# A trunk of dense blocks and a recurrence on one core: the recurrence starts after the seventh dense block, and the loads of its post-processing move behind a later chunk

## The chip, the cores and the metric

The kernel runs on one core of a Trainium2 chip. The metric is the device time of one execution, in microseconds (us), as the median of three runs. Every product is an fp32 product made of three faster ones: a matrix is split into a high part (hi) and a rest (lo), and hi·hi, hi·lo and lo·hi are summed.

## The reference, cut to what matters

Two residual layers over 1024 tokens of 1024 features. Layer 0 mixes with a gated MLP and pools, layer 1 with a recurrence over time (below); each is followed by a SwiGLU block with 2816 hidden features.

```python
def wkv7_scan(r, w, k, v, a, b):
    def step(state, inp):
        r_t, w_t, k_t, v_t, a_t, b_t = inp
        sa = jnp.einsum('bhvk,bhk->bhv', state, a_t)
        state = (state * w_t[:, :, None, :] + sa[..., None] * b_t[:, :, None, :]
                 + v_t[..., None] * k_t[:, :, None, :])
        return state, jnp.einsum('bhvk,bhk->bhv', state, r_t)
    _, ys = lax.scan(step, s0, xs)

# around it, per token and head
y = ((y - mean) * lax.rsqrt(var + GN_EPS)).reshape(bsz, seq, d)
y = y * ln_w + ln_b
y = (y + bonus.reshape(bsz, seq, d)) 
return (y * g) @ w_o, v_first

def swiglu(hn, w_gate, w_up, w_down):
    return (jax.nn.silu(hn @ w_gate) * (hn @ w_up)) @ w_down
```

## The kernel before, in words

The 1024 tokens are worked in two halves of 512, h = 0 and 1. The recurrence is computed in chunks of 64 tokens, eight per half, as matrix products of 64 by 64 within a chunk and a state handed from chunk to chunk. `recur(h, wp)` is its code. It runs in two phases, one for each half, and in each it is interleaved with dense work: `drive` takes steps of a SwiGLU generator (`ffn`) and, by a ratio of 3, steps of the recurrence. Each `yield` of the recurrence names a cost; a dense block (one 128-feature slice: 24 matmuls of 128 by 512, eight triples by `mm3`) counts 1, and so earns a cost of 3. PE's order is the order in which the code is written (and thus the costs at the `yield`s decide it); the order of the other engines is found by a planner that simulates the program's time. DVE, ACT and the queues run in order.

The dense blocks are of three kinds: gate (`sg`: the silu of its result), up (its result times `sg` gives `hidhi`, `hidlo`) and down (`wdhi`, `wdlo` times `hidhi`, `hidlo`, added to `h`). The weights of a block come by one load of 512 KB into `raw` (three buffers), issued on ACT's queue; ACT makes `whi` or `wdhi` of it, DVE `wlo` or `wdlo`.

SP's queue issues the loads of the recurrence. `load(c)` brings `ar`, `bk`, `uv` and `XT` of a chunk; `bk` has one buffer. `with_reload` puts four loads of two slices of `h` (512 KB each) between the first steps. `gram(c, q)` is 32 products of `ar` and `bk`, which DVE masks into `gt`; `flip_bk` transposes `bk`; `below` and `below2` finish the triangular inverse in `XT`; `burst(c)` then chains the products of a chunk: `Q`, then `uv`, then the new state `S`, with the two grams of the next chunk in between. `post(jj)` normalizes two finished chunks: it reads `lnw` (the weights of the norm), `vch` (v of the two chunks) and `gch` (the gate), makes `ysb`, and transposes it on PE. The order of the products of the recurrence on PE is kept by `ordered`, which puts each behind the last.

`tc.issue_after(i)` has an instruction stand behind instruction i in the order of the program; it is no wait for a result.

Of the kernel before, what the change touches and what calls it, by code (L numbers as in the profile page):

```python
# [16 lines left out]
P = 128  # L17
# [13 lines left out]
LOWRANK_AT, GATE_AT, MIX_AT = (5, 8), (7, 8), 2  # L31

BURST = 12.0

BESIDE = (4, 2)

# [2 lines left out]
def tile_trunk(  # L39
# [8 lines left out]
    act, dve, pool, pe, sp = nc.scalar, nc.vector, nc.gpsimd, nc.tensor, nc.sync  # L48
# [25 lines left out]
    def bc(ap, shape):  # L74
        return ap.to_broadcast(shape)
# [20 lines left out]
    def col(c):  # L96
        return vec[:, c : c + 1]
# [35 lines left out]
    def take(key):  # L133
        i = pos[0]
        assert plan[i][0] == key, (plan[i][0], key)
        pos[0] += 1
        split_at(i)
        load_at(i + 1)
        if i + 1 in raws:
            load_at(i + 2)  # L140
        split_at(i + 1)
        return ready.pop(i)
# [186 lines left out]
    def mmt():  # L329
        return pst("mm")  # L330

    def auxt():
        return pst("aux")
# [6 lines left out]
    def hsl(h):  # L340
        return slice(h * HT, (h + 1) * HT)

    def mm3(o, whi, wlo, xhi, xlo, first, last):
        pe.matmul(o, whi, xhi, start=first, stop=False)  # L344
        pe.matmul(o, whi, xlo, start=False, stop=False)  # L345
        pe.matmul(o, wlo, xhi, start=False, stop=last)  # L346

    def rsqrt(t):
        pool.tensor_tensor(out=t, in0=t, in1=mhalf[:, : t.shape[1]], op=ALU.pow)  # L349
# [125 lines left out]
    o = auxt()  # L475
# [3 lines left out]
    o = auxt()  # L479
# [19 lines left out]
    for h in range(2):  # L499
        ops = [mmt() for _ in range(4)]  # L500
        for kp in range(4):
            with tc.issue_after(x_issued):
                whi, wlo = take(("v0", h, kp))
            whi, wlo = (w.rearrange("p (k m) -> p k m", k=2) for w in (whi, wlo))
            xhi, xlo = hn[h]
# [25 lines left out]
    o = auxt()  # L531
# [36 lines left out]
    for m in ORD_Z:  # L568
        g = m - 8
        whi, wlo = take(("in", m))  # L570
        win = WINS[g]
        prev = None
        for h in range(2):
            o = mmt()
# [15 lines left out]
            while w < win:  # L590
                n = l0.tile([P, 16 + HT], F32, tag="zw", bufs=2, name="zw")
                b0 = base + w
# [12 lines left out]
    for m in range(4):  # L605
        whi, wlo = take(("in", m))
        for h in range(2):
            o = mmt()
# [7 lines left out]
    for h in range(2):  # L616
        hi, lo = act_tiles((xlp, actp)[h])
        ys.append((hi, lo))
        for k in (4, 5, 6, 7, 0, 1, 2, 3):
            src = zt[k - 4, h] if k >= 4 else mx[:, k, hsl(h)]  # L620
# [135 lines left out]
    g_d = [dram.tile([P, KT, HT], F32, name=f"g_d{h}") for h in range(2)]  # L756
    xi_d = [dram.tile([2, 8, 2, 8, 32, 2, 32], F32, name=f"xi_d{h}") for h in range(2)]
# [31 lines left out]
    rows = [slice(0, 64), slice(64, 128)]  # L789
# [354 lines left out]
    def recur(h, wp):  # L1144
# [5 lines left out]
        def wt(tag, bufs, shape):  # L1150
            return wp.tile(shape, F32, tag=tag, bufs=bufs, name=tag)
# [2 lines left out]
            return pst("sm").rearrange("p (a b) -> p a b", b=64)  # L1154

        lnw = wt("lnw", 1, [P, 8, 64])
        for r in range(2):
            act.dma_start(
                lnw[rows[r]], rwkv_ln_w[0].rearrange("(p r d) -> r p d", r=2, d=64)[r].partition_broadcast(64)
            )  # L1160
        C, ypair = {}, {}
        S, Q, last = [state_d], {}, []

        def ordered(f, *args, **kw):
# [16 lines left out]
        def load(c):  # L1181
            ar = wt("ar", 2, [P, 8, 2, 64])
            sp.dma_start(ar, ar_d[h][c])
            bk = wt("bk", 1, [P, 8, 2, 64])
            sp.dma_start(bk, bk_d[h][c])
            uv = wt("uv", 2, [P, 8, 2, 64])
            vs = v_d[h][c * 64 : c * 64 + 64]
            sp.dma_start(uv[64:128, :, 0, :], vs[:, 0])
            sp.dma_start(uv[0:64, :, 1, :], vs[:, 1])

            xx = wt("XT", 2, [P, 8, 96])
            x1, XT = xx[:, :, 0:32], xx[:, :, 32:96]
            for r in range(2):
                b0 = r * 64
                sp.dma_start(
                    xx[b0 : b0 + 32, :, 0:64], xi_d[h][0, :, r, c].rearrange("p i a j -> i p (a j)")
                )
                sp.dma_start(XT[b0 + 32 : b0 + 64, :, 32:64], xi_d[h][1, :, r, c, :, 1].rearrange("p i j -> i p j"))
                pool.memset(XT[b0 + 32 : b0 + 64, :, 0:32], 0.0)
            gt = wt("gt", 2, [P, 8, 2, P])  # L1200
            C[c] = (ar, bk, uv, gt, x1, XT)

        def gram(c, q):
            ar, bk, _, gt, _, _ = C[c]
            og = [pst("sm").rearrange("p (a b) -> p a b", b=P) for _ in range(2)]
            for j in range(4):
                p = q * 4 + j
                for b in range(2):
                    for r in range(2):
                        mm(  # L1210
                            og[r][rows[b], j, :], bk[rows[r], p, b, :],
                            ar[rows[r], p].rearrange("p a b -> p (a b)"), start=True, stop=True,
                        )
            for r in range(2):
                dve.tensor_tensor(
                    out=gt[:, q * 4 : q * 4 + 4, r, :], in0=og[r], in1=bc(gm.unsqueeze(1), [P, 4, P]), op=ALU.mult
                )
# [110 lines left out]
        def post(jj):  # L1328
            yp = ypair[0]
            j = h * 4 + jj  # L1330
            gch = wt("gch", 1, [P, 8, P])
            sp.dma_start(gch, g_d[h][:, :, jj * P : (jj + 1) * P])
            vch = wt("vch", 1, [P, 2, 8, 64])
            for r in range(2):
                sp.dma_start(
                    vch[rows[r]].rearrange("t c p d -> t c (p d)"),
                    v_d[h][jj * P : (jj + 1) * P, r].rearrange("(c t) p d -> t c (p d)", t=64),
                )
            v16 = vch.rearrange("t c p d -> t (c p) d")
            b16 = bon[:, 2 * j : 2 * j + 2, :].rearrange("t c p -> t (c p)")  # L1340
            pool.tensor_tensor(out=v16, in0=v16, in1=bc(b16.unsqueeze(2), [P, 16, 64]), op=ALU.mult)
            st = wt("st", 1, [P, 2, 8, 6])
            for r in range(2):
                for p in range(8):
                    dve.bn_stats(out=st[:, r, p, :], in_=yp[:, r, p, :])
            sts = st.rearrange("p a b s -> p (a b) s")
            mean, dm, var = (wt(n, 1, [P, 16]) for n in ("mean", "dm", "var"))
            me, mo, ve, vo = (sts[:, :, i] for i in (1, 4, 2, 5))
            dve.tensor_tensor(out=mean, in0=me, in1=mo, op=ALU.add)
            dve.tensor_tensor(out=dm, in0=me, in1=mo, op=ALU.subtract)  # L1350
            dve.tensor_tensor(out=var, in0=ve, in1=vo, op=ALU.add)
            dve.scalar_tensor_tensor(out=dm, in0=dm, scalar=16.0, in1=dm, op0=ALU.mult, op1=ALU.mult)
            dve.tensor_tensor(out=var, in0=var, in1=dm, op=ALU.add)
            dve.tensor_scalar(out=var, in0=var, scalar1=1.0 / 64, scalar2=GN_EPS, op0=ALU.mult, op1=ALU.add)
            rsqrt(var)
            dve.scalar_tensor_tensor(out=mean, in0=mean, scalar=-0.5, in1=var, op0=ALU.mult, op1=ALU.mult)
            yield 0.3
            ysb = wt("ysb", 1, [P, 2, 8, 64])
            for r in range(2):
                for p in range(8):  # L1360
                    i = r * 8 + p
                    act.activation(
                        ysb[:, r, p, :], yp[:, r, p, :], AF.Identity, scale=var[:, i : i + 1], bias=mean[:, i : i + 1]
                    )
            yield 0.3
            for q, eng in enumerate((dve, pool)):
                eng.tensor_tensor(out=ysb[:, q], in0=ysb[:, q], in1=lnw, op=ALU.mult)
                eng.tensor_tensor(out=ysb[:, q], in0=ysb[:, q], in1=vch[:, q], op=ALU.add)
            yield 0.3
            yield 0.3  # L1370
            for q in range(2):
                o = pst("sm")
                for i in range(4):
                    p = 4 * q + i // 2 * 2
                    ordered(
                        pe.transpose, o[:, i * P : (i + 1) * P], ysb[:, i % 2, p : p + 2, :].rearrange("t p d -> t (p d)"), ident
                    )
                ov = o.rearrange("p (q c r t) -> p q r c t", q=2, c=2, r=2)
                for i in range(4):
                    m = q * 4 + i  # L1380
                    g = gch[:, m, :].rearrange("p (c t) -> p c t", c=2)
                    dve.scalar_tensor_tensor(
                        out=g, in0=ov[:, i // 2, i % 2], scalar=col(C_LNB + m), in1=g, op0=ALU.add, op1=ALU.mult,
                    )
                yield 0.5
            sp.dma_start(y_d[h][:, :, jj * P : (jj + 1) * P], gch)

        load(0)
        load(1)
        yield 0.2  # L1390
        gram(0, 0)
        yield 0.5
        gram(0, 1)
# [4 lines left out]
        for c in range(8):  # L1398
            bkt, w1 = yield from burst(c, bkt, w1)
            yield BURST / 2  # L1400
            if c % 2 == 1:
                yield from post(c // 2)
            yield BURST / 2

# [219 lines left out]
```

## Time and profile before

| | |
|---|---|
| median of three runs | 2525.26 us (2524.75 to 2525.75) |
| the profiled execution | 2522.66 us |
| its span | 2520.9 us, mean granted clock of PE 0.983 |
| PE busy | 2432.2 us (96%) |
| DVE, ACT, POOL busy | 1401.8, 890.7, 299.8 us |
| moved by DMA | 310.69 MB, mean 123 GB/s |
| phase 1 of the recurrence, h = 0 | about 927 to 1240 us |
| phase 2, h = 1 | about 1669 to 1940 us |

A row of the profile gives start, length, engine, line of the kernel, operation, output <- inputs, and in brackets the idle time ahead of it with what ended it. Engines with a q (ACTq, SPq) are their queues, on which DMAs are issued. Buffer numbers are left out in the profile; in the order of the program they stand behind the names.

### The profile page before, as it was taken

The page shows a single profiled execution, that of the slowest core. Times are in us where ns is not written, and L with a number is a line of the kernel's source. Part 1 is how long each engine was busy: PE and PEld are TensorE (multiplying, and loading weights), DVE is VectorE, ACT ScalarE, POOL GpSimd, SP SyncE. Part 2 cuts the span into 40 slices and gives each one's busy share as a digit, 9 for nine tenths or more (in the row PEclk, how much of TensorE's full clock was granted, in tenths as well). Part 3 has the DMA queues.
Part 4 walks back from the last instruction along what each step waited for, and adds up shares of the span by engine and source line. Part 5 has one row for each costly group of instructions (what it writes and reads, how often), then busy time and mean ns, then how long its engine had stood idle before and what let it go on. Part 6 is the DMA issues. An engine that isn't in the chain of part 4 may idle for free.

```text
span 2520.9 us, 37945 instructions
## 1 busy us (share of the span) xinstructions
PE 2432.2 (96%) x15735; PEld 1983.2 (79%) x15735; DVE 1401.8 (56%) x2118; ACT 890.7 (35%) x1335; POOL 299.8 (12%) x298
## 2 busy tenths in 40 slices
PE   8999999999989998999999989899999999999998
PEld 6888888888767786788877667787888878888887
DVE  5445634444865873555457855964654445434443
ACT  6233322222544432333234643433333224323223
POOL 0200000000323410111001222401211000100001
PEclk9999999999999998999999999999999999999999
DMA  5113433323255478433334355585653332423331
GB/s 175 48 59 92 142 109 116 101 92 112 88 156 134 123 204 203 136 113 102 112 118 138 111 179 133 132 230 159 167 150 110 100 107 77 150 88 119 94 92 59
DMA packets 434956, 310.69 MB, mean 123 GB/s; under 512 B 93216, under 2 KB 395424, under 8 KB 433760
## 3 DMA queue, kind: packets, MB, share of 16 engines
q10 hardware_dynamic: 297280, 210.53, 27.9%
q1 hardware_dynamic: 137504, 97.75, 13.7%
q8 instruction: 123, 2.02, 0.3%
q14 instruction: 49, 0.40, 0.0%
HBM read 254.68 MB, written 53.54 MB: 122 GB/s over the span
## 4 chain that ended last, share of the span: by engine, by line
PE 74%; DVE 13%; DMA 7%; issue 3%; ACT 2%; POOL 1%; SPq 0%; ACTq 0%; DVEq 0%; POOLq 0%
PE mm L344 21%; PE mm L345 21%; PE mm L346 20%; PE sm L1168 4%; DVE wlo L146 2%; DMA raw<-in_ffn_w_up_dram 2%; DVE it L1117 1%; DVE mix L887 1%; DVE xi L1122 1%; DMA iat<-at_d 1%; PE yp L1168 1%; DMA raw<-in_ffn_w_down_dram 1%; PE mm L510 1%; PE mm L511 1%; ACT whi L145 1%
## 5 line engine op out<-in xcount | busy, mean ns | idle before, releaser
L344 PE MATMUL mm<-ahi,whi 128*128 128x512 f32 x1952 | 766.9, 394 | 5.1 <-DVE h L423 4.0
L345 PE MATMUL mm<-alo,whi 128*128 128x512 f32 x1952 | 769.1, 394 | 1.6 <-DVE alo L146 1.6
L346 PE MATMUL mm<-ahi,wlo 128*128 128x512 f32 x1952 | 766.5, 393 | 2.6 <-DVE wlo L146 2.6
L145 ACT ACTIVATE whi<-raw 128x1024 fp32r<-128x1024 f32 x288 | 304.3, 1058 | 768.1 <-PE mm L345 608.5
L146 DVE TENSOR_TENSOR wlo<-raw,whi 128x1024 fp32r<-128x1024 f32 x288 | 362.0, 1257 | 309.8 <-ACT whi L145 301.5
L344 PEld LDWEIGHTS mm<-ahi,whi 128*128 128x128 f32 x1952 | 367.9, 189 | 87.2 <-issue 4.5
L346 PEld LDWEIGHTS mm<-ahi,wlo 128*128 128x128 f32 x1952 | 368.2, 189 | 82.3 <-DVE wlo L146 3.4
L345 PEld LDWEIGHTS mm<-alo,whi 128*128 128x128 f32 x1952 | 368.2, 189 | 82.1 <-issue 3.7
L345 PE MATMUL mm<-hidlo,wdhi 128*128 128x512 f32 x624 | 246.6, 395 | 1.3 <-DVE hidlo L672 1.2
L344 PE MATMUL mm<-hidhi,wdhi 128*128 128x512 f32 x624 | 239.8, 394 | 6.6 <-ACT hidhi L671 5.2
L346 PE MATMUL mm<-hidhi,wdlo 128*128 128x512 f32 x624 | 245.5, 393 | 0.0
L423 DVE TENSOR_TENSOR h<-h,mm 128x512 f32<-128x512 f32 x192 | 129.2, 684 | 149.9 <-PE mm L346 149.1
L145 ACT ACTIVATE wdhi<-raw 128x1024 fp32r<-128x1024 f32 x82 | 86.6, 1059 | 254.9 <-DMA raw<-in_ffn_w_down_dram 150.8
L146 DVE TENSOR_TENSOR wdlo<-raw,wdhi 128x1024 fp32r<-128x1024 f32 x82 | 100.4, 1225 | 111.3 <-ACT wdhi L145 105.5
L668 DVE TENSOR_TENSOR sg<-sg,mm 128x512 f32<-128x512 f32 x88 | 60.2, 685 | 165.3 <-PE mm L346 164.9
L344 PEld LDWEIGHTS mm<-hidhi,wdhi 128*128 128x128 f32 x624 | 117.2, 188 | 35.2 <-ACT hidhi L671 7.4
L345 PEld LDWEIGHTS mm<-hidlo,wdhi 128*128 128x128 f32 x624 | 118.2, 189 | 27.9 <-DVE hidlo L672 3.2
L346 PEld LDWEIGHTS mm<-hidhi,wdlo 128*128 128x128 f32 x624 | 118.2, 189 | 24.6 <-issue 0.2
L423 DVE TENSOR_TENSOR hA<-hA,mm 128x512 f32<-128x512 f32 x72 | 48.7, 685 | 77.0 <-PE mm L346 77.0
L349 POOL TENSOR_TENSOR nrs<-nrs,small 128x4 f32<-128x4 f32 x8 | 10.0, 1246 | 625.4 <-DVE nrs L371 625.4
L344 PE MATMUL mm<-xhi,whi 128*128 128x512 f32 (+1 forms) x160 | 66.0, 412 | 4.2 <-ACT k L925 4.2
L672 DVE TENSOR_TENSOR hidlo<-sg,hidhi 128x512 fp32r<-128x512 f32 x88 | 64.5, 733 | 3.8 <-ACT hidhi L671 3.7
(300 smaller groups left out, 2952.1 us busy)
## 6 DMA issues: line engine op xcount, KB each, us to landing
raw<-in_ffn_w_gate_dram ACTq DMA_DIRECT2D x88, 512.0 KB
raw<-in_ffn_w_up_dram ACTq DMA_DIRECT2D x88, 512.0 KB
raw<-in_ffn_w_down_dram ACTq DMA_DIRECT2D x88, 512.0 KB
raw<-in_ab_w_in_dram ACTq DMA_DIRECT2D x16, 512.0 KB
raw<-in_ab_w_out_dram ACTq DMA_DIRECT2D x16, 512.0 KB
raw<-in_rwkv_w_k_dram ACTq DMA_DIRECT2D x16, 512.0 KB
raw<-in_rwkv_w_r_dram ACTq DMA_DIRECT2D x16, 512.0 KB
ar_d<-ar SPq DMA_DIRECT2D x16, 512.0 KB
```

Source lines behind the costliest of these rows:

```text
L145: act.activation(hi, src, AF.Copy)
L146: (eng or dve).tensor_tensor(out=lo, in0=src, in1=hi.bitcast(F32), op=ALU.subtract)
L344: pe.matmul(o, whi, xhi, start=first, stop=False)
L345: pe.matmul(o, whi, xlo, start=False, stop=False)
L346: pe.matmul(o, wlo, xhi, start=False, stop=last)
L423: dve.tensor_tensor(out=H[h][:, m, :], in0=H[h][:, m, :], in1=o, op=ALU.add)
L510: pe.matmul(ops[j], xhi[:, k, sl], whi[:, kk], start=(k == 0), stop=False)
L511: pe.matmul(ops[j], xhi[:, k, sl], wlo[:, kk], start=False, stop=False)
L668: dve.tensor_tensor(out=s, in0=s, in1=o, op=ALU.mult)
L672: dve.tensor_tensor(out=lo, in0=s, in1=hi.bitcast(F32), op=ALU.subtract)
L887: dve.scalar_tensor_tensor(out=t, in0=hn1[:, k, 0:HT], scalar=col(c), in1=t, op0=ALU.mult, op1=ALU.add)
L1168: i = f(*args, **kw)
```

## The change

The first step of the recurrence behind the loads of chunks 0 and 1 gets a cost of 21 instead of 0.2, seven dense blocks at the ratio of 3, and the first gram is ordered behind the last matmul of the seventh dense block. `lnw` is no longer loaded on ACT's queue at the start of `recur`, but on SP's in the first `post` of a phase. The loads of `lnw`, `vch` and `gch` are placed behind the last load of chunk 2, 4, 6 or 7, for the four `post`s of a phase.

```diff
+START = 21.0
...
     def mm3(o, whi, wlo, xhi, xlo, first, last):
         pe.matmul(o, whi, xhi, start=first, stop=False)
         pe.matmul(o, whi, xlo, start=False, stop=False)
-        pe.matmul(o, wlo, xhi, start=False, stop=last)
+        dense_last[0] = pe.matmul(o, wlo, xhi, start=False, stop=last).ins
...
         lnw = wt("lnw", 1, [P, 8, 64])
-        for r in range(2):
-            act.dma_start(
-                lnw[rows[r]], rwkv_ln_w[0].rearrange("(p r d) -> r p d", r=2, d=64)[r].partition_broadcast(64)
-            )
-        C, ypair = {}, {}
+        C, ypair, issued = {}, {}, {}
...
-                sp.dma_start(XT[b0 + 32 : b0 + 64, :, 32:64], xi_d[h][1, :, r, c, :, 1].rearrange("p i j -> i p j"))
+                i = sp.dma_start(XT[b0 + 32 : b0 + 64, :, 32:64], xi_d[h][1, :, r, c, :, 1].rearrange("p i j -> i p j"))
...
+            issued[c] = i.ins
...
             gch = wt("gch", 1, [P, 8, P])
-            sp.dma_start(gch, g_d[h][:, :, jj * P : (jj + 1) * P])
             vch = wt("vch", 1, [P, 2, 8, 64])
+
+            behind = issued[min(2 * jj + 2, 7)]
+
+            def dma(dst, src):
+                nonlocal behind
+                with tc.issue_after(behind):
+                    behind = sp.dma_start(dst, src).ins
+
+            if jj == 0:
+                for r in range(2):
+                    dma(lnw[rows[r]], rwkv_ln_w[0].rearrange("(p r d) -> r p d", r=2, d=64)[r].partition_broadcast(64))
             for r in range(2):
-                sp.dma_start(
+                dma(
                     vch[rows[r]].rearrange("t c p d -> t c (p d)"),
                     v_d[h][jj * P : (jj + 1) * P, r].rearrange("(c t) p d -> t c (p d)", t=64),
                 )
+            dma(gch, g_d[h][:, :, jj * P : (jj + 1) * P])
...
         load(0)
         load(1)
-        yield 0.2
+        yield START
+        last.append(dense_last[0])
         gram(0, 0)
```

On PE, at the first gram of phase 1 (`sm<-ar,bk`). Before, it stood inside the fifth dense block, a gate or up block:

```order
L346 MATMUL mm_7500<-ahi_6621,wlo_7461 128x512
L344 MATMUL mm_7500<-ahi_6621,whi_7460 128x512
L345 MATMUL mm_7500<-alo_6622,whi_7460 128x512
L346 MATMUL mm_7500<-ahi_6621,wlo_7461 128x512
L344 MATMUL mm_7500<-ahi_6621,whi_7460 128x512
L1170 MATMUL sm_7072<-ar_7041,bk_7043 64x128
L1168 MATMUL sm_7073<-ar_7041,bk_7043 64x128
```

Now, inside the eighth, with two down blocks under way:

```order
L349 MATMUL mm_7318<-hidlo_7195,wdhi_7302 128x512
L350 MATMUL mm_7318<-hidhi_7194,wdlo_7303 128x512
L348 MATMUL mm_7318<-hidhi_7263,wdhi_7308 128x512
L348 MATMUL mm_7405<-hidhi_7125,wdhi_7269 128x512
L349 MATMUL mm_7405<-hidlo_7126,wdhi_7269 128x512
L349 MATMUL mm_7318<-hidlo_7264,wdhi_7308 128x512
L350 MATMUL mm_7318<-hidhi_7263,wdlo_7309 128x512
L1168 MATMUL sm_7329<-ar_7039,bk_7041 64x128
L1168 MATMUL sm_7330<-ar_7039,bk_7041 64x128
```

The gram moved from behind 109 dense matmuls of the phase to behind 179; the first matmul that reads `hidhi_7263` stands five rows ahead of it.

On SP, from the load of chunk 1 to `bk` of chunk 1 and chunk 2's loads. Before:

```order
L1195 DMA XT<-xi_d_1939 32x8x64
L1198 DMA XT<-xi_d_1939 32x8x32
L1474 DMA h<-h_d_81 128x1024 x3
L1332 DMA gch<-g_d_1937 128x8x128
L1335 DMA vch<-v_d_1933 64x2x512 x2
L1185 DMA bk<-bk_d_1931 128x1024
L1195 DMA XT<-xi_d_1939 32x8x64
L1198 DMA XT<-xi_d_1939 32x8x32
L1195 DMA XT<-xi_d_1939 32x8x64
L1198 DMA XT<-xi_d_1939 32x8x32
L1183 DMA ar<-ar_d_1929 128x1024
```

Now:

```order
L1487 DMA h<-h_d_81 128x1024 x4
L1185 DMA bk<-bk_d_1931 128x1024
L1195 DMA XT<-xi_d_1939 32x8x64
L1198 DMA XT<-xi_d_1939 32x8x32
L1195 DMA XT<-xi_d_1939 32x8x64
L1183 DMA ar<-ar_d_1929 128x1024
L1198 DMA XT<-xi_d_1939 32x8x32
L1340 DMA lnw<-in_rwkv_ln_w_dram 64x8x64 x2
L1340 DMA vch<-v_d_1933 64x2x512 x2
L1340 DMA gch<-g_d_1937 128x8x128
L1188 DMA uv<-v_d_1933 64x8x64
L1189 DMA uv<-v_d_1933 64x8x64
```

`gch` and `vch` moved from ahead of `bk` of chunk 1 to behind `XT` of chunk 2, with `lnw` ahead of them; `uv` and then `bk` of chunk 2 follow.

On DVE, around the first masking (`gt`) of phase 1. Before:

```order
L146 TENSOR_TENSOR wdlo_7816<-raw_7780,wdhi_7815 128x1024
L1215 TENSOR_TENSOR gt_7055<-sm_7072,gm_1945 128x4x128
L1215 TENSOR_TENSOR gt_7055<-sm_7073,gm_1945 128x4x128
L146 TENSOR_TENSOR wdlo_7822<-raw_7813,wdhi_7821 128x1024
L146 TENSOR_TENSOR wlo_7828<-raw_7819,whi_7827 128x1024
L1215 TENSOR_TENSOR gt_7055<-sm_7096,gm_1945 128x4x128
```

Now:

```order
L148 TENSOR_TENSOR wdlo_7309<-raw_7300,wdhi_7308 128x1024
L148 TENSOR_TENSOR wlo_7315<-raw_7306,whi_7314 128x1024
L672 TENSOR_TENSOR sg_7229<-sg_7229,mm_7237 128x512
L676 TENSOR_TENSOR hidlo_7264<-sg_7229,hidhi_7263 128x512
L148 TENSOR_TENSOR wlo_7703<-raw_7312,whi_7702 128x1024
L427 TENSOR_TENSOR h_7037<-h_7037,mm_7318 128x512
L148 TENSOR_TENSOR wlo_7739<-raw_7700,whi_7738 128x1024
L1216 TENSOR_TENSOR gt_7053<-sm_7329,gm_1945 128x4x128
```

The splits of weights that stood between the maskings now stand ahead of the first of them; one (`wlo_7315`) stands ahead of the product `sg_7229` that `hidhi_7263` is made of.

On DVE, in the second burst of phase 1 (chunk 1), from its `Q` on. Before:

```order
L1278 TENSOR_TENSOR Q_7598<-akv_7579,sm_7581 128x512
L423 TENSOR_TENSOR h_7037<-h_7037,mm_7949 128x512
L1215 TENSOR_TENSOR gt_7384<-sm_7603,gm_1945 128x4x128
L1215 TENSOR_TENSOR gt_7384<-sm_7604,gm_1945 128x4x128
L1286 COPY uv_7060<-sm_7623 64x8x64
L1215 TENSOR_TENSOR gt_7384<-sm_7658,gm_1945 128x4x128
L1215 TENSOR_TENSOR gt_7384<-sm_7659,gm_1945 128x4x128
L1307 TENSOR_TENSOR Q_7699<-S_7317,sm_7682 128x512
```

Now:

```order
L1279 TENSOR_TENSOR Q_7840<-akv_7821,sm_7823 128x512
L148 TENSOR_TENSOR wdlo_8151<-raw_8055,wdhi_8150 128x1024
L1216 TENSOR_TENSOR gt_7635<-sm_7842,gm_1945 128x4x128
L1216 TENSOR_TENSOR gt_7635<-sm_7843,gm_1945 128x4x128
L1287 COPY uv_7058<-sm_7862 64x8x64
L148 TENSOR_TENSOR wdlo_8203<-raw_8148,wdhi_8202 128x1024
L1216 TENSOR_TENSOR gt_7635<-sm_7900,gm_1945 128x4x128
L1216 TENSOR_TENSOR gt_7635<-sm_7901,gm_1945 128x4x128
L1308 TENSOR_TENSOR Q_7938<-S_7571,sm_7921 128x512
L148 TENSOR_TENSOR wdlo_8209<-raw_8200,wdhi_8208 128x1024
```

Three splits of down weights came into this burst's chain, where additions to `h` stood. The same holds for the fifth burst of phase 1 and the second of phase 2.

More of the change, by code (lines that the diff above doesn't have):

```diff
@@ L341, in hsl @@
         return slice(h * HT, (h + 1) * HT)
+    dense_last = [None]
     def mm3(o, whi, wlo, xhi, xlo, first, last):
```

## The prediction, made before the changed kernel ran

> **What bounds the kernel now.** I read the page's head and its chain first, then stretches of the two recurrence phases, then the waits and the rows of TensorE (PE) there.
>
> ```profile
> span 2520.9 us, 37945 instructions
> PE 2432.2 (96%) x15735; PEld 1983.2 (79%) x15735; DVE 1401.8 (56%) x2118; ACT 890.7 (35%) x1335; POOL 299.8 (12%) x298
> ```
>
> PE is busy for 96% of the span, and the change takes no product away. So all that it can win or lose is PE idle time and PE clock. The whole idle time is 2520.9 - 2432.2 = 88.7 us; only the part in the two recurrence phases (927 to 1240 and 1669 to 1940 us) is touched. The next view cuts their openings, and one later place, into 10 us stretches; the column after the engines is the granted clock, then the DMA share and the GB/s.
>
> ```profile
> 940.00:950.00 10.00, 10.00 (x46) 8.29 (x45) 3.37 (x4) 2.58 (x4) 0.00 (x0) 1.00 0.89 239
> 950.00:960.00 10.00, 8.12 (x58) 6.29 (x57) 3.65 (x4) 2.24 (x3) 0.00 (x0) 0.83 1.00 248
> 960.00:970.00 10.00, 8.21 (x57) 6.40 (x56) 3.65 (x4) 2.60 (x3) 0.00 (x0) 0.83 1.17 255
> 970.00:980.00 10.00, 8.94 (x70) 7.05 (x69) 4.51 (x6) 4.17 (x6) 0.00 (x0) 1.00 1.15 282
> 980.00:990.00 10.00, 6.06 (x107) 4.48 (x106) 3.87 (x6) 2.55 (x5) 1.90 (x1) 0.82 0.74 203
> 990.00:1000.00 10.00, 10.00 (x236) 8.70 (x234) 5.29 (x8) 1.63 (x3) 0.61 (x2) 0.84 0.28 77
> 1050.00:1060.00 10.00, 9.89 (x149) 8.00 (x150) 4.45 (x8) 1.46 (x3) 0.00 (x0) 0.83 0.90 237
> 1700.00:1710.00 10.00, 7.39 (x60) 5.60 (x58) 2.75 (x4) 2.60 (x3) 0.00 (x0) 1.00 1.13 305
> 1710.00:1720.00 10.00, 8.53 (x58) 6.88 (x59) 4.96 (x7) 3.75 (x6) 0.49 (x1) 0.66 1.15 275
> ```
>
> From 940 to 980 the DMA engines are full (shares 0.89 to 1.17), and PE loses time in every stretch from 950 on. Its rows there, with the idle time before them in brackets, and two pairs of neighbours that give the spacing of dense matmuls:
>
> ```profile
> 927.27 0.39 PE L344 MATMUL mm<-ahi,whi 128*128 128x512 f32 x1
> ...
> 928.63 0.39 PE L344 MATMUL mm<-ahi,whi 128*128 128x512 f32 x1
> ...
> 954.02 0.29 PE L1170 MATMUL sm<-ar,bk 64*64 64x128 f32 x1 [1.88 <-DMA bk<-bk_d]
> ...
> 957.18 0.63 PE L344 MATMUL mm<-ahi,whi 128*128 128x512 f32 x1
> 957.61 0.63 PE L345 MATMUL mm<-alo,whi 128*128 128x512 f32 x1
> ...
> 964.60 1.10 PE L1168 MATMUL sm<-ar,bk 64*64 64x128 f32 x30 [1.79 <-DVE gt L1215]
> ...
> 973.53 0.66 PE L1168 MATMUL sm<-ident,bk 128*128 128x128 f32 x4 [1.06 <-DVE gt L1215]
> ...
> 987.95 0.69 PE L1168 MATMUL sm<-ar,bk 64*64 64x128 f32 x2 [3.94 <-DVE XT L1256]
> ...
> 1050.11 0.43 PE L1168 MATMUL sm<-ar,bk 64*64 64x128 f32 x2 [2.64 <-DVE gt L1215]
> ...
> 1711.47 1.12 PE L1168 MATMUL sm<-ident,bk 128*128 128x128 f32 x4 [4.08 <-DVE gt L1215]
> ...
> 1725.09 0.43 PE L1168 MATMUL sm<-ar,bk 64*64 64x128 f32 x2 [0.79 <-DVE XT L1256]
> ```
>
> Phase 1's opening idles 1.88 + 1.79 + 1.06 + 3.94 = 8.7 us. Dense matmuls stand 1.36 / 6 = 0.227 us apart at full clock and 0.43 after an idle stretch; the clocks 0.83, 0.83, 0.82 and 0.84 are (0.17 + 0.17 + 0.18 + 0.16) x 10 = 6.8 us more. Together 15.5 us. Phase 2's opening: 4.08 + 0.79 idle and 3.4 of clock (0.66), 8.3 us. The openings hold 23.8 us.
>
> What was late there, by the chain of waits (start, length):
>
> ```profile
> 941.96 12.21 DMA lnw<-in_rwkv_ln_w_dram
> ...
> 955.04 9.08 DMA ar<-ar_d
> ...
> 970.13 14.14 DMA raw<-in_ffn_w_up_dram
> ...
> 1708.08 13.34 DMA raw<-in_ffn_w_up_dram
> ```
>
> And two rows of ScalarE (ACT), whose queue issues the loads of weights and, at the start of a phase, of lnw:
>
> ```profile
> 941.96 3.58 ACTq L1158 DMA_DIRECT2D lnw<-in_rwkv_ln_w_dram  x2
> ...
> 945.59 0.60 ACT L661 ACTIVATE sg<-mm 128x512 f32<-128x512 f32 x1 [4.52 <-issue]
> ```
>
> Transfers of 9 to 14 us, and instructions of the in-order ACT and VectorE (DVE) behind them. The gram products' masks (gt) are not slow; they stand on DVE behind the splitting of weights that have not landed.
>
> **The change, part by part.** *Loads.* lnw (0.25 MB), vch and gch (0.5 MB each) leave the opening: 1.25 MB, at the 255 GB/s of 960 to 970 some 4.9 us of full DMA engines, and 3.58 us of issuing on ACT. They come back behind the load of chunk 2 (lnw only in the first post-processing of each phase), and of chunks 4, 6 and 7. There they stand on SP's in-order queue ahead of bk of the chunk. What that does in the first:
>
> ```profile
> 970.24 1.43 SPq L1335 DMA_DIRECT2D vch<-v_d  x2
> ...
> 999.73 0.57 SPq L1185 DMA_DIRECT2D bk<-bk_d  x1
> ...
> 1006.82 0.38 PE L1168 MATMUL sm<-ar,bk 64*64 64x128 f32 x2
> ```
>
> bk of chunk 2 is issued at 999.73 and first used at 1006.82, 7.1 us later. Five issues of about 0.7 us (1.43 / 2) and 1.25 MB go ahead of it: 3.5 us if the transfers overlap the issues, 4.9 if they do not. A quiet 512 KB load takes 3.4 us (below), so 6.9 to 8.3 us: a wait of 0 to 1.2 us per phase. With a clock drop the worst is 2 x 2.9 = 6. I take 0.5 in all. Later bk loads have the same margin and 0.25 MB less ahead; I take nothing.
>
> *Later start.* The recurrence starts 70 dense matmuls later (179 instead of 109 of its phase): moved work, no added work. It ends later by the same, with over 400 dense matmuls of the phase left behind the last post-processing, so the end costs nothing.
>
> *The opening after.* The grams now stand behind the seventh block, so their masks wait for weights that have been split. In exchange the dense blocks themselves can wait. The order puts, on DVE, the split of the next up weights ahead of the product that makes hid of the last hidden block, and PE needs that hid after 174 dense matmuls, at 927.27 + 174 x 0.227 = 966.8. The raw load of those weights is issued on ACT behind the landing of ar of chunk 1. That landing, 964.1 now (955.04 + 9.08), comes earlier as the 12.21 us landing of lnw that held SP goes: I take 961.5. The load then shares the engines with the four pieces of h. Bounds of its length are a quiet one (issue at 1136.77 and use at 1140.20, 3.4 us) and the full one of 14.14:
>
> ```profile
> 1136.77 0.35 ACTq L115 DMA_DIRECT2D raw<-in_ffn_w_down_dram  x1
> ...
> 1140.20 1.06 ACT L145 ACTIVATE wdhi<-raw 128x1024 fp32r<-128x1024 f32 x1 [2.48 <-DMA raw<-in_ffn_w_down_dram]
> ```
>
> I take 9, near the 9.08 of ar, since h is still there and 1.25 MB is not. It lands at 970.5; then 1.06 (whi) + 1.24 (wlo) + 0.68 (sg) + 0.63 (hidhi) and gaps, about 3.9. PE goes on at 974.4, 7.6 us late, and the slow clock behind adds 2.2 (about 11 matmuls 0.2 later). Phase 1's opening then costs 9.8 instead of 15.5: a gain of 5.7, with bounds 15.5 - 1.9 = 13.6 (quiet) and 15.5 - 14.9 = 0.6 (full). Phase 2 begins, and issues ar of chunk 1, here:
>
> ```profile
> 1669.13 0.39 PE L344 MATMUL mm<-ahi,whi 128*128 128x512 f32 x1
> ...
> 1694.87 0.34 SPq L1183 DMA_DIRECT2D ar<-ar_d  x1
> ```
>
> That is 25.7 us after the first matmul (27.8 in phase 1). With lnw gone I let ar be issued 3.5 us sooner, at 1691.4, and land 9.1 later, at 1700.5; the load takes 9 x 255 / 305 = 7.5 (the engines moved 305 GB/s from 1700 to 1710) and lands at 1708. With 3.9 behind it that is 1711.9, against PE's 1669.13 + 39.5 = 1708.6: a wait of 3.3 and 1.9 of clock, 5.2 for 8.3, a gain of 3.1; bounds 8.3 (quiet) and 0 (a load of 13.34, wait 9).
>
> *The bursts after.* The later start also shifts which splits of weights fall into which burst. In three bursts (phase 1's second and fifth, phase 2's second) the down weights are now loaded inside the burst and their splits stand on DVE ahead of gt or of the new state. The trace has one such place now:
>
> ```profile
> 1041.41 1.06 ACT L145 ACTIVATE wdhi<-raw 128x1024 fp32r<-128x1024 f32 x1 [4.40 <-DMA raw<-in_ffn_w_down_dram]
> ...
> 1045.41 1.06 ACT L145 ACTIVATE wdhi<-raw 128x1024 fp32r<-128x1024 f32 x1 [2.45 <-DMA raw<-in_ffn_w_down_dram]
> ...
> 1046.49 1.23 DVE L146 TENSOR_TENSOR wdlo<-raw,wdhi 128x1024 fp32r<-128x1024 f32 x1 [1.45 <-ACT wdhi L145]
> ...
> 1049.37 1.28 DVE L1215 TENSOR_TENSOR gt<-sm,gm 128x512 f32<-128x512 f32 x2
> ```
>
> ACT waits for raw, DVE for ACT, gt stands behind, PE waits 2.64 (at 1050.11) and the clock of 1050 to 1060 (0.83) adds 1.7: 4.3 us. Three times that is 12.9; the place itself goes (-4.3), as the order there changes. In the remaining bursts I assume no difference. So +8.6, with bounds -4.3 (none of the three waits) and +15 (each at 6.5 as two waits fall into one burst). Since DMA is quieter there than at 1050 (0.90), I take two thirds of it, +5.7.
>
> In a sentence apart: the Trainium skill, in "TensorE: Matmul & The Clock Gate", section "HAM oscillation — how this bites in real kernels", says that it is idle gaps over about 3.4 us that gate the clock; by it two thirds of three times 1.7 in the bursts and the 1.9 of phase 2 fall away, and the sum would be 5.3 lower. The trace disagrees: after only 1.88 us idle at 954.02 the spacing is 0.43.
>
> Sum: -5.7 - 3.1 + 0.5 + 5.7 = -2.6 us on the profiled execution. That one took 2522.66 us (its span and 1.8 around it), 2.6 below the median of 2525.26, which I carry over: 2525.26 - 2.6, about 2522.7.
>
> **The rivals.** *A: the openings' waits vanish.* The load of up weights finds the engines nearly free and the bursts' waits are half hidden. For it: 1.25 MB less just there. Against: h (2 MB) is still in the same 10 us. Gains 13.6 + 8.3, bursts at +3 or less: 2503 to 2509, say 2506. In sentences apart: the Trainium skill, "DMA: Bandwidth & Descriptors", "Queues, rings and completion order", has the DMA engines take turns between the queues by packet. The load on ACT's queue would then get half of 255 GB/s, 512 KB in about 4.1 us, and with 1.4 of fixed time land near 967, for a total near 2518. The 14.14 us row speaks against an even share.
>
> *B: slower.* One mechanism: the weight loads issued inside the bursts. With three raw buffers, each next load waits for a split, which on DVE stands behind the burst's own steps. From the point where each of the three bursts costs more than about 6.5 us and the first block's wait is near its upper bound (a load of about 13 us), it decides: 15 - 0.6 - 3 + 0.5, some +12: 2537.
>
> *C: bk late.* The five loads ahead of bk make the burst's second gram wait 1.2 us and more with a clock drop, in both phases: +6 instead of +0.5: 2528.
>
> **How the numbers follow.** A change of 0.2% (5 us: below 2520.2, above 2530.3) is about what a measurement of this kernel can tell from none. The forecast with its own range 2516 to 2529 has a chance of 0.45: 0.13 of it under 2520.2, 0.32 within. A has 0.26, all faster. B has 0.22, all but 0.02 slower. C has 0.07: 0.03 within, 0.04 slower. So faster 0.39, same 0.37, slower 0.24. For 8 in 10 the range reaches to the middle of A and of B: 2506 to 2536.
>
> **What would show it.** Right: at the first gram of each phase no wait for gt, bk or XT, one wait of PE for hidhi of 5 to 10 us shortly before it (about 967), one of about 3 in phase 2, and waits of 1 to 3 us for gt in three bursts at a clock near 0.83. Wrong: no wait for hidhi (A), waits for bk at the second burst (C), or waits of over 4 us for gt or the state in several bursts (B). A slower or faster stretch outside the two phases would have no place in this sum.

## The result: 0.8% slower, and the profile after

The changed kernel takes 2543.16 us (2540.06 to 2547.64), the kernel before 2525.01 beside it: a ratio of 1.0078, with a 95% interval of 1.0066 to 1.009. It is 18 us slower, 20 above the forecast and 7 above the range's end. The page's head of the profiled execution:

```profile
span 2541.2 us, 37955 instructions
PE 2441.9 (96%) x15735; PEld 1991.0 (78%) x15735; DVE 1402.6 (55%) x2118; ACT 891.3 (35%) x1335; POOL 300.2 (12%) x298
```

PE does the same 15735 matmuls. Of the 20.3 us between the spans, 10.6 are idle (99.3 for 88.7) and 9.7 are busy time. Most of the busy time is a slower clock: the mean granted clock of 0.980, for 0.983 before, accounts for some 8 us. Where the losses lie is seen in four windows, the two openings and what follows each. The first four rows are the kernel before, in each the length, PE's busy time and then, behind the engines, the granted clock, the DMA share and the GB/s:

```profile
920.00:1000.00 80.00, 71.32 (x654) 57.76 (x652) 43.17 (x74) 23.85 (x32) 3.73 (x7) 0.91 0.79 204
1000.00:1260.00 260.00, 253.99 (x2989) 210.85 (x2990) 141.19 (x279) 81.19 (x156) 32.43 (x25) 0.99 0.39 114
1660.00:1730.00 70.00, 65.11 (x528) 52.74 (x530) 40.75 (x72) 22.92 (x30) 3.07 (x5) 0.95 0.84 226
1730.00:2000.00 270.00, 269.67 (x3169) 225.11 (x3164) 149.03 (x290) 88.12 (x164) 34.59 (x26) 1.00 0.45 130
```

The changed kernel:

```profile
920.00:1000.00 80.00, 79.20 (x648) 64.69 (x648) 47.10 (x83) 23.79 (x31) 1.83 (x6) 1.00 0.65 185
1000.00:1260.00 260.00, 240.31 (x2962) 198.95 (x2959) 135.03 (x272) 80.31 (x153) 36.06 (x26) 0.95 0.43 117
1660.00:1730.00 70.00, 68.02 (x322) 55.65 (x321) 46.95 (x88) 25.02 (x30) 1.22 (x4) 0.98 0.86 239
1730.00:2000.00 270.00, 260.75 (x3331) 216.72 (x3330) 142.64 (x285) 82.27 (x160) 35.72 (x28) 0.99 0.43 126
```

A window's loss is its idle time and (1 - clock) x length. Phase 1's opening goes from 8.7 + 7.2 = 15.9 to 0.8, phase 2's from 4.9 + 3.5 = 8.4 to 2.0 + 1.4 = 3.4: the openings gain 20 us. Behind them phase 1 goes from 6.0 + 2.6 = 8.6 to 19.7 + 13.0 = 32.7, and phase 2 from 0.3 to 9.3 + 2.7 = 12.0: 36 lost. (The clock has two digits, so each of the long windows is good to 1 or 2 us.) That is 16 of the 20.3; the rest lies outside the windows, some 3 of it as idle time between 600 and 920 us, ahead of both phases. PE's longest waits in the windows:

```profile
970.05 0.73 PE L348 MATMUL mm<-hidhi,wdhi 128*128 128x512 f32 x2 [0.80 <-ACT hidhi L675]
...
1016.06 0.65 PE L1168 MATMUL sm<-ar,bk 64*64 64x128 f32 x2 [6.08 <-DMA bk<-bk_d]
...
1045.57 0.40 PE L1168 MATMUL sm<-ident,ysb 128*128 128x128 f32 x1 [2.53 <-DVE ysb L1380]
...
1078.22 0.40 PE L1168 MATMUL sm<-ar,bk 64*64 64x128 f32 x2 [3.36 <-DMA bk<-bk_d]
...
1123.53 1.71 PE L1168 MATMUL sm<-ident,bk 128*128 128x128 f32 x8 [2.55 <-DVE gt L1216]
...
1136.27 0.24 PE L1168 MATMUL sm<-XT,w 32*32 32x32 f32 x2 [3.26 <-ACT w L1242]
...
1721.14 0.96 PE L348 MATMUL mm<-hidhi,wdhi 128*128 128x512 f32 x2 [1.98 <-ACT hidhi L675]
...
1765.07 0.40 PE L1168 MATMUL sm<-ar,bk 64*64 64x128 f32 x2 [1.35 <-DMA bk<-bk_d]
...
1775.26 1.15 PE L1168 MATMUL sm<-uv,bkt 128*64 128x64 f32 x32 [1.70 <-DVE uv L1287]
...
1782.03 0.69 PE L1168 MATMUL sm<-XT,gt 32*32 32x32 f32 x32 [2.04 <-DVE Q L1308]
...
1828.85 0.40 PE L1168 MATMUL sm<-ar,bk 64*64 64x128 f32 x2 [2.22 <-issue]
...
1870.55 0.43 PE L1168 MATMUL sm<-ar,bk 64*64 64x128 f32 x2 [1.94 <-DVE gt L1216]
```

Behind the openings two kinds stand out: bk of a chunk that is late (6.08, 3.36, 1.35; for the 2.22 at the same product the trace names no releaser), and DVE or ACT late behind splits of down weights in the fifth burst of phase 1 and the second and fifth of phase 2. For the first, SP's queue at the load of chunk 2, and bk's two late landings in the chain:

```profile
1000.55 1.29 SPq L1340 DMA_DIRECT2D lnw<-in_rwkv_ln_w_dram  x2
1001.88 1.28 SPq L1340 DMA_DIRECT2D vch<-v_d  x2
1003.21 0.60 SPq L1340 DMA_DIRECT2D gch<-g_d  x1
1003.92 1.85 SPq L1188 DMA_DIRECT2D uv<-v_d  x1
1005.81 0.81 SPq L1189 DMA_DIRECT2D uv<-v_d  x1
1006.72 2.83 SPq L1185 DMA_DIRECT2D bk<-bk_d  x1
```

```profile
1006.72 9.21 DMA bk<-bk_d
...
1068.93 9.16 DMA bk<-bk_d
```

bk is issued behind the five loads and `uv`; its issue alone takes 2.83 us, for 0.57 in the kernel before, and it lands 9.2 us after the issue's start, behind their bytes and beside a load of weights. From the first of the five issues to bk's landing it is 15.4 us. PE had finished the work ahead of it at 1010.

### The profile page after: what moved, and what is told of

Read it like the earlier page. It is cut to its first block, busy times and chain, and to the rows that moved or that the text cites. A ratio compares the mean times of both kernels' runs of the same rounds, so it can differ in the third digit from the quotient of the medians.

```text
span 2541.2 us, 37955 instructions
## 1 busy us (share of the span) xinstructions
PE 2441.9 (96%) x15735; PEld 1991.0 (78%) x15735; DVE 1402.6 (55%) x2118; ACT 891.3 (35%) x1335; POOL 300.2 (12%) x298
## 4 chain that ended last, share of the span: by engine, by line
PE 75%; DVE 11%; DMA 7%; ACT 3%; issue 2%; POOL 1%; SPq 0%; ACTq 0%; POOLq 0%; DVEq 0%
PE mm L348 21%; PE mm L350 21%; PE mm L349 21%; PE sm L1168 4%; DVE wlo L148 2%; DMA raw<-in_ffn_w_down_dram 2%; DMA bk<-bk_d 1%; DVE mix L891 1%; DVE it L1121 1%; DVE xi L1126 1%; PE yp L1168 1%; DMA raw<-n_d 1%; DMA iat<-at_d 1%; ACT whi L147 1%; DMA raw<-y_d 1%
## 5 line engine op out<-in xcount | busy, mean ns | idle before, releaser
L348 PEld LDWEIGHTS mm<-ahi,whi 128*128 128x128 f32 x1952 | 369.0, 189 | 88.7 <-issue 5.3
```

## The experiments

The change has two parts, and the traces offer two causes. *Theory bk*: the loads now stand ahead of bk. *Theory weights*: the later start puts the bursts where the down weights are loaded and split. Of the first four runs two keep one part each, and two place the loads of lnw, vch and gch behind bk, one with each start. Each edit also has the planner order the engines anew, so two kernels can differ by more than the edit; where that bears on a reading, it is said.

**The later start alone** (`start_only`): before, with (cut: `START = 21.0` and `dense_last`, as in the change)

```diff
-        yield 0.2
+        yield START
+        last.append(dense_last[0])
```

> The later start alone: the first gram behind the seventh dense block, the loads of lnw, vch and gch where they were before. Theory bk (the loads placed ahead of bk of chunks 2, 4 and 6 make bk late, and the cost of the change is theirs): no wait for bk over 1 us in the trace, and 10 to 18 us less than the changed kernel, 2525 to 2533 us. Theory weights (the later start brings the splits of down weights into the bursts, and the cost is the start's): the waits for gt, w, uv and Q of the changed kernel (2.55, 3.48, 1.70, 2.04) stay and the time is 2536 to 2543.

2538.74 us, ratio 1.0046 (1.0028 to 1.0064) to before. No wait for bk, but waits for gt of 3.18, 2.65 and 2.44, for Q of 4.21 and for uv of 3.82. Theory weights has its part: the start costs 12 us with the loads where they were. In the two openings PE waits 4.39 and 2.75 us for hidhi, for 0.80 and 1.98 in the changed kernel: there the moved loads help.

**The loads alone** (`loads_only`): the changed kernel, with

```diff
-        yield START
-        last.append(dense_last[0])
+        yield 0.2
```

> The early start of before, with the loads of lnw, vch and gch behind the load of chunks 2, 4, 6 and 7. Theory bk: a wait for bk of 3 to 7 us at the second burst and 1 to 4 us at the fourth, bought with a shorter opening: 2525 to 2535. Theory weights: the opening is shorter by 5 to 10 and the rest as before: 2513 to 2520.

2535.17 us, 1.0035 (1.0022 to 1.0048): theory bk has its part too. The long waits are all at the first gram matmul of a chunk whose bk stands behind the extra loads:

```profile
1000.45 0.40 PE L1168 MATMUL sm<-ar,bk 64*64 64x128 f32 x2 [3.29 <-issue]
...
1056.23 0.66 PE L1168 MATMUL sm<-ar,bk 64*64 64x128 f32 x2 [3.15 <-issue]
...
1742.39 0.66 PE L1168 MATMUL sm<-ar,bk 64*64 64x128 f32 x2 [3.86 <-DMA bk<-bk_d]
...
1850.61 0.40 PE L1168 MATMUL sm<-ar,bk 64*64 64x128 f32 x2 [2.37 <-DMA bk<-bk_d]
```

In the first two the trace names no releaser; they stand at the same product as the others, and I count them to bk.

**The loads behind bk** (`behind_bk`: the changed kernel; `behind_bk_early`: the same with the early start):

```diff
-            sp.dma_start(bk, bk_d[h][c])
+            ibk = sp.dma_start(bk, bk_d[h][c])
...
-            issued[c] = i.ins
+            issued[c] = ibk.ins
```

> The changed kernel with the same loads placed behind bk of the chunk and no longer ahead of it. Theory bk: waits of PE for bk (10.8 us and some 4 of slow clock) fall to under 2: 2526 to 2532. Theory weights: bk's wait is only taken over by the down weights that come at the same time: 2536 to 2543.

> The early start of before, with the loads of lnw, vch and gch behind bk of chunks 2, 4, 6 and 7. Both theories: no wait for bk, opening shorter by 5 to 12 us than before: 2513 to 2521. Were it slower than before, the post-processing or the weights would be late behind these loads, and neither theory would do.

With the early start: 2514.62 us, 0.9947 (0.9929 to 0.9965), 12 us faster than before and 20.6 faster than with the loads ahead of bk. With the late start: 2544.36, 1.0069 (1.0052 to 1.0086), no gain in the total. Theory bk's forecast for `behind_bk` fails. Its trace shows what took bk's place in the burst that had waited 6.08:

```profile
1000.04 0.57 SPq L1185 DMA_DIRECT2D bk<-bk_d  x1
...
1005.64 0.35 ACTq L117 DMA_DIRECT2D raw<-in_ffn_w_down_dram  x1
...
1012.45 1.06 ACT L147 ACTIVATE wdhi<-raw 128x1024 fp32r<-128x1024 f32 x1 [5.28 <-DMA raw<-in_ffn_w_down_dram]
...
1013.54 1.23 DVE L148 TENSOR_TENSOR wdlo<-raw,wdhi 128x1024 fp32r<-128x1024 f32 x1 [5.44 <-ACT wdhi L147]
1014.68 1.28 DVE L1216 TENSOR_TENSOR gt<-sm,gm 128x512 f32<-128x512 f32 x2
...
1015.42 0.43 PE L1168 MATMUL sm<-ar,bk 64*64 64x128 f32 x2 [3.21 <-DVE gt L1216]
```

bk goes out before the other loads and in time; the down weights, issued in the burst at 1005.64, are split at 1012.45, 6.8 us later; DVE holds gt behind their split, and PE waits for gt. Two more such loads follow in the burst. Here the two delays lie side by side, and taking one away uncovers part of the other: 3.21 of 6.08.

The six kernels as a table (us; rows the start, columns the place of the three loads):

| | as before | ahead of bk | behind bk |
|---|---|---|---|
| early start | 2525 to 2526 (before) | 2535.2 | 2514.6 |
| START = 21 | 2538.7 | 2543.2 (the change) | 2544.4 |

That is not the whole account of `behind_bk`. The start of the first dense matmul of each phase cuts the span of an execution at points that are the same in every kernel (us, one execution each):

| | up to phase 1 | phase 1 to phase 2 | from phase 2 on |
|---|---|---|---|
| before | 927.3 | 741.9 | 851.8 |
| `loads_only` | 929.6 | 741.0 | 864.2 |
| `behind_bk_early` | 929.6 | 730.3 | 853.5 |
| the change | 929.7 | 749.9 | 861.6 |
| `behind_bk` | 926.5 | 741.6 | 872.6 |

With the early start the loads ahead of bk cost 10.7 us in each phase. At 21 they cost 8.3 in phase 1, and in phase 2 the kernel with the loads behind bk is the slower, by 11.0. "No gain" is the sum of the two. The pair at 21 is not like for like in phase 2. Counted in the rows of PE, the third to sixth bursts begin their first `Q` product behind 403, 429, 530 and 563 dense matmuls of the phase in the changed kernel, and behind 378, 404, 494 and 522 in `behind_bk`; in phase 1, and in both phases of the early pair, the two kernels of a pair agree within 3. So the bursts fall in another place. In the fifth of `behind_bk` three splits of down weights stand between its first `Q` and its new state, where the changed kernel has one and waits 1.94 in all:

```profile
1857.49 1.23 DVE L148 TENSOR_TENSOR wdlo<-raw,wdhi 128x1024 fp32r<-128x1024 f32 x1 [3.52 <-ACT wdhi L147]
...
1859.49 0.90 PE L1168 MATMUL sm<-ident,bk 128*128 128x128 f32 x3 [3.09 <-DVE gt L1216]
...
1863.44 1.23 DVE L148 TENSOR_TENSOR wdlo<-raw,wdhi 128x1024 fp32r<-128x1024 f32 x1 [3.41 <-ACT wdhi L147]
...
1865.32 1.07 PE L1168 MATMUL sm<-XT,gt 32*32 32x32 f32 x32 [3.86 <-DVE Q L1308]
```

That the place of the bursts makes the 11 us is likely by theory weights, but no run has the loads behind bk at the changed kernel's places.

**Is it the late start as such, or where the bursts fall?** A group of three hidden blocks is 216 dense matmuls, nine blocks. If the place in that rhythm decides, a start one whole group later must wait as little as the early one. The later starts need the four loads of h ahead of the first down block, so in two later starts and in a control at 21 the code issues h right behind chunk 1 (without it, starts of 24, 30 and 40 would read h before it is loaded and gave no time; 24 was not tried again). The loads stand behind bk as above, and START is 21, 30 or 40:

```diff
-        yield START
+        for _ in range(3):
+            yield 0.1
+        yield START - 0.3
```

> The control of the three runs with a later start: loads behind bk, START = 21, and the four loads of h issued right behind the load of chunk 1, with no dense block between them (the later starts need h that early). Bursts as with the loads behind bk at 21, which took 2544.4. Both theories: 2538 to 2547; h is only moved by some us in an opening that waits 1 to 4 us.

> The loads behind bk, h right behind chunk 1, and START = 30 (ten blocks instead of seven). Theory alignment (a late start costs only by the place in the weights' rhythm at which the bursts fall; a group of three hidden blocks takes nine blocks): at 30 no burst of phase 1 issues a load of weights and splits the same weights, and only two of phase 2 do: 2510 to 2524. Theory late start (the later the first gram, the more is lost, since the dense work behind it has less slack): slower than at 21, 2545 to 2560.

> The loads behind bk, h right behind chunk 1, and START = 40: every gram stands 207 to 239 dense matmuls behind its place with the early start, about one full group of nine blocks (216). Theory alignment: the bursts wait as with the early start, which took 2514.6: 2508 to 2522. Theory late start: 2550 to 2570.

| START, loads behind bk | us | ratio to before |
|---|---|---|
| 21 (control) | 2547.01 | 1.0092 (1.0077 to 1.0107) |
| 30 | 2536.36 | 1.0051 (1.0035 to 1.0067) |
| 40 | 2521.78 | 0.9985 (0.997 to 1.0) |

At 40, about a group behind the early start, the time is 25 us below that at 21, and at the end of the range that theory alignment gave; it is still 7 above the early start. That a late start costs as such is refuted. At 30 the total misses what theory alignment expected, by 12 us, and the two phases say why. The windows behind the openings, of 21 and then of 30:

```profile
1000.00:1260.00 260.00, 243.91 (x3035) 201.88 (x3027) 136.99 (x277) 82.08 (x155) 36.54 (x26) 0.97 0.44 122
...
1730.00:2000.00 270.00, 254.04 (x3256) 211.40 (x3255) 137.58 (x279) 80.78 (x157) 37.01 (x28) 0.96 0.44 124
```

```profile
1000.00:1260.00 260.00, 255.87 (x3316) 212.90 (x3315) 145.52 (x289) 88.32 (x166) 36.70 (x28) 0.99 0.46 130
...
1730.00:2000.00 270.00, 252.99 (x3261) 210.14 (x3254) 136.06 (x281) 84.02 (x162) 34.42 (x28) 0.96 0.44 126
```

In phase 1, where by the order no burst issues and splits the same weights, idle time falls from 16.1 to 4.1 us. In phase 2, where two bursts do (three weights and two), it is 17.0, for 16.0 at 21. I had priced such a pair of bursts far too low: some 13 of the 17 idle lie in or right behind them (waits of 1.99, 1.24, 4.89, 1.66 and 3.24), with some 10 of clock in the window. The profiled execution of 30 took 2544.55, 8 above its median, so these figures are rather high. The number of such bursts in a phase goes with its loss; how one makes PE wait is shown by the rows of `behind_bk` above.

**Does bk cost again where the bursts fall well?** (`xth_s40`: START = 40, the loads ahead of bk.)

> START = 40 with h right behind chunk 1 and the loads behind the last XT load of the chunk, ahead of its bk, as in the changed kernel. Theory alignment: with the bursts back in a good place the lateness of bk costs in full again, as it did with the early start (2535.2 against 2514.6): 15 to 22 us over the same start with the loads behind bk, 2527 to 2542. Theory late start: as with the changed kernel, within 2 us of the other placement at 40, 2550 to 2570.

2540.92 us, 1.0067 (1.0052 to 1.0082): 19.1 over the same start with the loads behind bk, about as with the early start (20.6). The bursts of this pair stand behind the same dense matmuls in both phases. Where bk comes late again:

```profile
1048.72 0.65 PE L1168 MATMUL sm<-ar,bk 64*64 64x128 f32 x2 [4.63 <-issue]
...
1790.88 0.65 PE L1168 MATMUL sm<-ar,bk 64*64 64x128 f32 x2 [3.87 <-DMA bk<-bk_d]
```

**How much may stand ahead of bk** (`gch_behind`: early start, lnw and vch ahead of bk, gch behind):

```diff
+            behind = behind_bk
             dma(gch, g_d[h][:, :, jj * P : (jj + 1) * P])
```

> The early start, lnw and vch behind the last XT load (ahead of bk of the chunk), gch alone moved behind bk. It stands between the runs with all three ahead of bk (2535.2) and all three behind (2514.6). If the lateness of bk is the cost and goes with what stands ahead of it on SP, 0.75 instead of 1.25 MB in the first case and 0.5 instead of 1 later: 2519 to 2529, with waits for bk of about half (3.29, 3.15, 3.86, 2.37 with all ahead). If it is the place of gch's load or its contention with the weights that matters, not bk: 2514 to 2518 or 2533 to 2537.

2518.56 us, 0.9969 (0.9956 to 0.9982): 3.9 over all behind, which is not clear of noise, and 16.6 under all ahead. About half the bytes cost a fifth or less, so bk seems to have some slack. The result lies between the two ranges expected, 0.4 us below that of theory bk and 0.6 above that of its rival. The waits at the gram speak for bk: where they were 3.29, 3.15, 3.86 and 2.37, they are 1.23 (for Q), 3.02, 1.44 and under 0.6.

**A start a little later, loads behind bk** (`bk_s15`): `START = 15.0`.

> The loads behind bk, START = 15 (five blocks): the first gram stands 17 dense matmuls later than with the early start. Theory alignment: bursts in nearly the same place as with the early start, fewer splits of weights in them (1 and 0 in phase 1, 1 and 2 in phase 2, by the order), opening shorter by 2 to 5: 2508 to 2518. Theory late start (2514.6 at 0.2 and 2544.4 at 21, in line between the two from the grams' shift of 17 and 73 matmuls): 2520 to 2524.

2505.97 us, 0.9919 (0.9905 to 0.9933): the fastest of all, 20 us below before, 37 below the change and 2 below the range of theory alignment. It still waits in the openings (5.62 and 4.01), and little behind them:

```profile
968.14 1.98 PE L1168 MATMUL sm<-ar,bk 64*64 64x128 f32 x30 [5.62 <-DVE gt L1216]
...
1693.80 1.78 PE L1168 MATMUL sm<-ar,bk 64*64 64x128 f32 x30 [4.01 <-DVE gt L1216]
...
1842.60 1.26 PE L1168 MATMUL sm<-ident,bk 128*128 128x128 f32 x8 [2.20 <-DVE gt L1216]
```

Its opening is not the shorter one that I expected of it; the bursts are. By the windows the openings lose 14 us, for 7 with the early start, and the bursts 5, for 11. These cancel, so where the 9 us between the two medians are won these traces do not show.

## Why the prediction was wrong, by its steps

**The openings.** The wait came where I had put it; its size was wrong. The chain of the changed kernel and PE's wait at its end (0.80, above):

```profile
954.20 5.06 DMA ar<-ar_d
...
959.34 4.29 DMA raw<-in_ffn_w_up_dram
```

The raw load goes out behind ar (959.3; I had 961.5), lands after 4.3 us (I had 9, by ar's old landing), and hidhi is ready 0.8 late and not 7.6. Phase 2 has the same wait, 1.98 for my 3.3. The nearest row for the load's length was the quiet one of 3.4. The openings gained 20, not 8.8. Rival A was right on them. The Trainium skill ("DMA: Bandwidth & Descriptors", "Queues, rings and completion order") has the DMA engines take turns between the queues; my estimate by it, a landing near 967 and some 5.5 us after issue, was nearer than the 9, though still too long.

**bk.** This term failed most. I took 0.5 us in all; the runs give 20.6 (early start), 19.1 (START = 40) and 8.3 (START = 21, phase 1 alone) for the loads ahead of bk against behind. The step that failed: I let bk land a quiet 3.4 us behind the five issues or their bytes, 6.9 to 8.3 in all, bounded the wait at 1.2 and left the later chunks at nothing. It took 15.4 from the first issue. The trace has landings of 9.21 and 9.16, in the second and the fourth burst alike. The nearer row was that of ar in the opening (9.08), a load on SP's queue among others, which I used for the weights; for bk I took the quiet one. Rival C named the mechanism; its price of 6 was under a third of it.

**The bursts.** Named rightly (phase 1's second and fifth, phase 2's second; phase 2's fifth came on top), and too small. With the loads behind bk, START = 21 costs 29.7 us over the early start, though its openings lose no more. The prediction had +8.6 and then took two thirds, because the DMA engines are quieter there; but the moved loads come into that quiet: from 1000 to 1010 us the DMA share is 1.03, for 0.28 before. The weights took 6.8 us (`behind_bk`, second burst) and 9.1 (the change, fifth burst) instead of 3.4. My reason for the discount was what the change takes away.

**The sum.** In phase 1, where the bursts of the two kernels at 21 stand in the same place, the measured parts nearly add: -11.6 for the loads out of the opening (`behind_bk_early` to before), 10.7 for their place ahead of bk and 11.3 for the start with the loads behind bk make 10.4, and the change costs 8.0. In phase 2 they make 31.5 (1.7, 10.7 and 19.1) for a cost of 9.8, but there the 19.1 belongs to bursts that stand elsewhere. So it was the sizes of the terms that failed, less the adding. Rival B, at 2537, had the right sign and the weights in the bursts; the wait near its upper bound that it also needed, in the opening, did not come.

**The clock.** By the rule of the Trainium skill ("TensorE: Matmul & The Clock Gate", "HAM oscillation — how this bites in real kernels") idle gaps under some 3.4 us would cost no clock. The changed kernel's 2.53 at 1045.57 is followed by matmuls 0.43 apart, and the clock makes up a good third to a half of the added time (8 by the mean granted clock, at most 9.7 by busy time, of 20.3). The trace disagrees with the rule again.

## What to carry to other kernels

Before a load is moved behind another on an in-order queue, look at what stands behind that place and when it is needed: the bytes now ahead of it count, not only their issues, and a single-buffered operand that is loaded just in time has almost no room. Work that is started later meets another part of its neighbour's rhythm, so judge a start by where every later step falls, and try several. And undo each part with the other both present and gone, and see that nothing else moved: here one placement of loads was worth 20 us with the early start and nothing in the total at 21, where it won 8 in one phase and the bursts had moved in the other.

## What the runs showed that I had not expected

A load of 512 KB behind 1 to 1.25 MB of its own queue took 9.2 us to land in two bursts, against 3.4 for a quiet one; in an opening whose engines moved over 300 GB/s a load on the other queue landed in 4.3:

```profile
950.00:960.00 10.00, 10.00 (x45) 8.27 (x45) 4.81 (x5) 3.70 (x4) 0.00 (x0) 1.00 1.12 304
960.00:970.00 10.00, 9.25 (x41) 7.32 (x39) 3.11 (x4) 3.24 (x5) 0.00 (x0) 1.00 1.13 333
```

Full DMA engines alone do not make a load late. Nor is it only what stands ahead on its own queue: in the fifth burst of phase 1 weights went out on ACT's queue when the load before them had landed, at a DMA share of 1.11, just behind the issues of vch, gch and uv on SP's:

```profile
1122.79 9.14 DMA raw<-in_ffn_w_down_dram
```

What sets the length of a load among others is left open. Nor does each idle gap cost clock: after 1.35, 1.70 and 2.22 us at 1765, 1775 and 1829 the clock stayed at 1.00, after 1.79 and 1.88 in the kernel before it fell. So the length of the gap does not decide alone; what does was not tried.
